# A hybrid decoder layer on one core: the Mixer's first projections on x without 1/rms, the last norm in a written order, one statistic moved

## The chip, the cores and the metric

The kernel runs on one core of a Trainium2 chip. The metric is the device time of one execution in microseconds; the time before is the median of three runs.

## The reference

x is 1024 positions of 1024 channels, all in float32. One layer is

```
x = x + 0.5 * SwiGLU_1(RMSNorm(x))
x = x + W_out concat[ GLA heads(RMSNorm(x)), short-conv groups(RMSNorm(x)) ]
x = x + 0.5 * SwiGLU_2(RMSNorm(x))
return RMSNorm(x)

RMSNorm(x)  = x * rsqrt(mean(x*x) + 1e-6) * gain
SwiGLU(h)   = (silu(h @ w_gate) * (h @ w_up)) @ w_down          # width 2816
proj        = h @ w_in  ->  q, k, v, g, a_lr, u, gate_b, gate_c
logg        = log_sigmoid(a_lr @ w_a2 + b_a) / 16               # the decay
o           = gated linear attention of q, k, v, logg, in chunks of 64; normed, times silu(g)
z           = gate_b * causal_conv(gate_c * u)                  # 3 taps
```

The layer is run once (DEPTH is 1). What matters below: 1/rms is one number per position and multiplies h, so it can be multiplied into a projection's result as well as into its operand.

## The kernel before, in words

x lies in SBUF as eight tiles of 128 channels by 1024 positions (`xs`), and the work goes over two halves of 512 positions. Every product is made of three TensorE passes: both operands are split into a high and a low part, and hi*hi, hi*lo and lo*hi are added (`PASSES`). A split is one cast on ScalarE (`S.copy`) and one subtraction, on VectorE as a rule.

Three stages follow each other. **FFN1** (class `Ffn`) runs its products in blocks of Strassen's form; its last block, `down_last` (L787 on), runs plainly: for half 0 and then half 1, over eight groups d of 128 channels, six matmuls of 128x512 each, then VectorE adds 0.5 times the sum to x (L802). The **Mixer** makes for each half: the decay (`project_decay`), k, q, v, u/c/b of the convolution, g, and the attention between them; then `out_proj` (L1203). **FFN2** is like FFN1, with the final norm at the end. Its `down_last` goes over three ranges of positions, 512, 256 and 256 wide (`tail`).

A norm is the class `Norm`. `add(k)` squares x's tile k on ScalarE and adds it to a running sum; the engine of the sum is `chain` (V is VectorE, G is GpSimd, none is VectorE and GpSimd in turns). `fin` then puts the sum through TensorE against ones (the statistic, L326), takes rsqrt on VectorE and GpSimd, spreads it as a diagonal (dg, L343) and multiplies that with ones on TensorE (rb, L347), which leaves 1/rms in every partition. `raw` (L355) multiplies x, gain and 1/rms in one VectorE instruction; `norm_h` splits the result into h's two parts.

The order of the work is made in three ways. A counter of modelled time, `clock`, is moved on by `tick(us)` after each step, and generators that were `spawn`ed with a wait are resumed when it has passed (`finish` resumes all to their ends). `pump` takes steps from a list of weight loads and splits as buffers come free: `plan_unit` puts a load (SyncE's queue), a cast (ScalarE) and a subtraction (VectorE) on it for each weight unit. Then a scheduler orders what each engine got, except where `in_order` pins the written order. At the end of FFN1, `finish()` and `in_order(f1.end, ...)` close the stage before the Mixer is built: half 0's norm is spawned 4.0 us after its last block, half 1's when the Mixer starts.

At the change from Mixer to FFN2 half 0 is normed beside `out_proj` of half 1, and `second` makes half 1's norm and operands while FFN2's first matmuls (`plain`, L482) run on half 0. At the end of FFN2 the three ranges are normed in turn: `first` multiplies range 0 on GpSimd (L1357), `scaled` multiplies ranges 1 and 2 on VectorE, `store` issues the transfers of the result on the queues of SyncE and ScalarE by turns.

Of the kernel before, what the change touches and what calls it, by code (L numbers as in the profile page):

```python
# [14 lines left out]
ALU = mybir.AluOpType  # L15
# [40 lines left out]
def trunk(ctx: ExitStack, tc: tile.TileContext, a, out):  # L56
# [60 lines left out]
    def pump(n=None):  # L117
        while todo and n != 0:
            n = n and n - 1
            tag, step = todo[0]  # L120
            if not tag():
                return
            todo.popleft()
            step()
# [81 lines left out]
    def plan_unit(src):  # L206

        st = {}
        key = ("u", units[0])
        units[0] += 1  # L210

        def load():
            st[0] = room("wr", "raw")
            nc.sync.dma_start(out=st[0], in_=src)

        def high():
            st[1] = room("wo", "whi", F32R)
            S.copy(st[1], st[0])  # L218

        def low():  # L220
            lo = room("wo", "wlo", F32R)
            sub(V, lo, st[0], st[1].bitcast(F32))
            free("wr")
            ready[key] = (st[1], lo)

        todo.extend([(room_for("wr"), load), (room_for("wo"), high), (room_for("wo"), low)])

    units, taken = [0], [0]
# [16 lines left out]
    def tick(us):  # L245
        pump()
# [41 lines left out]
    class Norm:  # L288
# [22 lines left out]

        def sum(self):
# [15 lines left out]
        def fin(self, bank, keep=True, waits=(2.7, 1.3), fill=lambda: None):  # L328

            n = self.n  # L330
            while self.late:
                self.sum()
# [37 lines left out]
    class Ffn:  # L370
# [411 lines left out]
        def down_last(self, after, ranges):  # L782
# [4 lines left out]
            rts = [[operand("ao", "act", x) for x in (r11, r21)], [operand("ao", "act", r12), None]]  # L787
            for n, (c, w) in enumerate(ranges):
                h, o = divmod(c, HALF)
                for d in range(KT):  # L790
                    if n == 1 and d == 0:
                        rts[1][1] = operand("ao", "act", r22)
# [13 lines left out]
                    tick(1.36 * w / HALF)  # L806
# [28 lines left out]
    def mixer_plans():  # L835
# [8 lines left out]
        for n in range(2):  # L844
            if n == 1:
                conv(0)
            group("k")
            group("q")
            for kq in range(4):
                plan_unit(a["w_v"][kq])  # L850
            if n == 0:
                conv(0)
            conv(1)
            group("g", 0)
            group("g", 1)
# [6 lines left out]
    class Mixer:  # L862
        def __init__(self, es):
            pool = lambda n, b, **k: es.enter_context(tc.tile_pool(name=n, bufs=b, reuse_waits="tile", **k))
            self.gp, self.sp = pool("gp", 9), pool("sp", 2)
            self.pp = pool("pp", 8, space=bass.MemoryType.PSUM)
# [12 lines left out]
            G.memset(self.state, 0.0)  # L879

# [25 lines left out]
        def project_decay(self, h):  # L906
# [237 lines left out]
        def attention(self, n, r):  # L1144
            yield 0.0
# [25 lines left out]
        def mix(self, n, h, front):  # L1171
# [9 lines left out]
            dec = self.project_decay(h)  # L1181
            next(dec)
            r["k"] = self.project_fm("k", h)
            r["b"] = next(dec)
            r["q"] = self.project_fm("q", h)
            spawn(self.attention(n, r))
# [27 lines left out]
    def norm_h(norm, h, bank, keep=True):  # L1214

        yield from norm.fin(bank, keep)
        hi, lo = (hp.tile([P, KT, HALF], F32R, tag="h", name=nm("h")) for _ in range(2))
# [40 lines left out]
    n2 = [Norm(0), Norm(HALF, chain=G)]  # L1258
# [43 lines left out]
    em = ExitStack()  # L1302
    m = Mixer(em)
    spawn(norm_h(n2[1], hm[1], m.bank), 3.0)
# [18 lines left out]
    m.out_proj(1, m1["act"], to_ffn2)  # L1323
    finish()
# [4 lines left out]
    f2.side = second(f2, n3[1], 0.0)  # L1329
    spawn(f2.side)  # L1330

    def store(n, k, y):

        c, w = tail[n]
# [123 lines left out]
```

## Time and profile before

| | |
|---|---|
| median of 3 runs | 1793.51 us (1792.5 to 1793.72) |
| the profiled execution's own time | 1794.18 us |
| its span in the profile | 1792.4 us, granted clock 0.983 |
| PE (TensorE matmul) busy | 1740.0 us, 97% |
| DVE (VectorE) busy | 1373.2 us, 77% |
| ACT (ScalarE) busy | 830.8 us, 46% |
| POOL (GpSimd) busy | 627.3 us, 35% |
| chain of work that ended last | PE 89%, issue 5%, DVE 4%, ACT 1%, POOL 1% |

All times are in microseconds from the span's start. "L802" is line 802 of the kernel. A view by windows gives busy time of each engine in a stretch, with the number of instructions in brackets, then TensorE's granted clock as a share of full speed. The timeline gives an engine's instructions in order, with the idle time ahead of each and what released it in square brackets. A PE that counts as busy isn't thereby at full speed: the granted clock tells that.

### The profile page before, as it was taken

Reading aid. Unit: us, or ns where it says so; the run is one execution under the profiler, and the core shown is the slowest. Engines: PE = TensorE matmul, PEld = TensorE weight load, DVE = VectorE, ACT = ScalarE, POOL = GpSimd, SP = SyncE. Lnnn points to the kernel's source line nnn. Section 1 sums busy time; section 2 is a strip of 40 time slices with the busy share of each in tenths; the row PEclk is TensorE's granted clock in tenths of the full one; section 3 lists DMA queues with packets and bytes.
Section 4 is the critical chain, followed back from the end, with each engine's and each line's share of the span. In section 5 each row is a group of like instructions: output and inputs, shape, how many; then the busy total and the mean of one; then the engine's idle time right before and its main releaser. Section 6 shows DMA issues by size and latency. Waiting matters only on the chain.

```text
span 1792.4 us, 21018 instructions
## 1 busy us (share of the span) xinstructions
PE 1740.0 (97%) x7814; PEld 1432.2 (80%) x7814; DVE 1373.2 (77%) x1847; ACT 830.8 (46%) x1442; POOL 627.3 (35%) x425
## 2 busy tenths in 40 slices
PE   8989999999999998899999999999999999999995
PEld 7768888888888875788888887888888888888884
DVE  6898778877798775775746668787788777987786
ACT  5464445554455444432442444354455544554453
POOL 0044354534444242220211020533545344543533
PEclk9999999999999998999999999999999999999997
DMA  5011212111111211222222222112111111112102
GB/s 214 1 47 47 71 47 63 54 49 61 58 48 47 71 53 47 83 83 82 70 84 90 77 73 92 34 36 71 48 59 52 55 59 59 47 48 71 48 24 94
DMA packets 35110, 112.92 MB, mean 63 GB/s; under 512 B 4384, under 2 KB 6848, under 8 KB 35008
## 3 DMA queue, kind: packets, MB, share of 16 engines
q1 hardware_dynamic: 32944, 108.42, 19.0%
q10 hardware_dynamic: 2064, 3.16, 0.5%
q8 instruction: 61, 1.00, 0.2%
q14 instruction: 41, 0.34, 0.1%
HBM read 107.37 MB, written 4.19 MB: 62 GB/s over the span
## 4 chain that ended last, share of the span: by engine, by line
PE 89%; issue 5%; DVE 4%; ACT 1%; POOL 1%; DMA 0%; ACTq 0%; POOLq 0%; DVEq 0%
PE ps L364 41%; PE ps L779 20%; PE pj L898 12%; PE dn L1203 5%; PE ps L482 2%; PE v L953 2%; PE ps L799 2%; PE sc L1022 1%; PE ps L506 1%; DVE sq L88 1%; PE alr L916 0%; DVE x L715 0%; DVE hraw L355 0%; DVE act L85 0%; DVE x L802 0%
## 5 line engine op out<-in xcount | busy, mean ns | idle before, releaser
L364 PE MATMUL ps<-R,w 128*128 128x512 f32 x1872 | 443.9, 391 | 3.4 <-DVE x L715 2.4
L364 PEld LDWEIGHTS ps<-R,w 128*128 128x128 f32 x1872 | 352.8, 189 | 78.0 <-DVE x L715 2.8
L779 PE MATMUL ps<-act,w 128*128 128x512 f32 x1680 | 386.3, 390 | 0.7 <-DVE x L715 0.7
L779 PEld LDWEIGHTS ps<-act,w 128*128 128x128 f32 x1680 | 313.7, 188 | 70.1 <-DVE act L701 4.4
L85 DVE TENSOR_TENSOR w<-raw,w 128x512 fp32r<-128x512 f32 x311 | 292.3, 946 | 78.7 <-ACT w L92 78.7
L364 PE MATMUL ps<-S,w 128*128 128x512 f32 x1404 | 331.4, 389 | 1.2 <-ACT w L92 1.2
L364 PEld LDWEIGHTS ps<-S,w 128*128 128x128 f32 x1404 | 263.6, 188 | 56.8 <-ACT w L92 1.7
L85 POOL TENSOR_TENSOR raw<-raw 128x512 f32<-128x512 f32 x59 | 77.3, 1309 | 597.4 <-DVE w L85 597.4
L92 ACT CAST w<-raw 128x512 fp32r<-128x512 f32 x311 | 192.2, 619 | 174.9 <-POOL raw L85 75.9
L88 POOL TENSOR_TENSOR x<-x,dx 128x512 f32<-128x512 f32 x160 | 265.7, 1697 | 17.5 <-ACT dx L766 17.5
L715 DVE SCALAR_TENSOR_TENSOR x<-ps,x 128x512 f32<-128x512 f32 x320 | 210.2, 682 | 20.7 <-PE ps L779 20.7
L898 PE MATMUL pj<-h,whi 128*128 128x512 f32 x640 | 200.4, 394 | 0.0
L85 DVE TENSOR_TENSOR wlo<-raw,whi 128x1024 fp32r<-128x1024 f32 x64 | 80.8, 1262 | 88.9 <-PE pj L898 47.4
L898 PEld LDWEIGHTS pj<-h,whi 128*128 128x128 f32 x640 | 119.0, 189 | 26.4 <-issue 1.9
L85 DVE TENSOR_TENSOR w<-T,w 128x512 fp32r<-128x512 f32 x118 | 102.4, 868 | 38.1 <-ACT w L92 38.1
L218 ACT CAST whi<-raw 128x1024 fp32r<-128x1024 f32 x64 | 67.0, 1046 | 138.7 <-PE pj L898 81.8
L898 PE MATMUL pj<-h,wlo 128*128 128x512 f32 x320 | 124.9, 390 | 0.0
L85 DVE TENSOR_TENSOR act<-act,act 128x512 fp32r<-128x512 f32 x103 | 109.8, 1069 | 13.1 <-ACT act L92 13.1
L92 ACT CAST act<-act 128x512 fp32r<-128x512 f32 x103 | 63.7, 621 | 75.7 <-PE ps L779 46.9
L92 ACT CAST w<-T 128x512 fp32r<-128x512 f32 x118 | 73.3, 621 | 53.6 <-PE ps L364 32.0
L85 POOL TENSOR_TENSOR raw<-raw,raw 128x512 f32<-128x512 f32 x59 | 95.5, 1619 | 4.6
L85 DVE TENSOR_TENSOR T<-raw,raw 128x512 f32<-128x512 f32 x59 | 49.5, 840 | 53.0 <-POOL raw L85 53.0
(196 smaller groups left out, 2152.3 us busy)
## 6 DMA issues: line engine op xcount, KB each, us to landing
raw<-in_ffn_w SPq DMA_DIRECT2D x86, 512.0 KB, 3.6
raw<-in_ffn_wd SPq DMA_DIRECT2D x44, 512.0 KB, 3.7
raw<-in_w_fm SPq DMA_DIRECT2D x40, 512.0 KB, 3.5
raw<-in_w_out SPq DMA_DIRECT2D x16, 512.0 KB, 3.6
x<-in_x SPq DMA_DIRECT2D x16, 256.0 KB, 6.1
raw<-in_w_v SPq DMA_DIRECT2D x8, 512.0 KB, 3.5
raw<-in_ffn_w ACTq DMA_DIRECT2D x2, 512.0 KB, 6.0
out<-y SPq DMA_DIRECT2D x2, 512.0 KB, 2.8
```

The source lines that it names most:

```text
L85: eng.tensor_tensor(o, x, y, op=ALU.subtract)
L88: eng.tensor_tensor(o, x, y, op=ALU.add)
L92: S.copy(hi, src)
L218: S.copy(st[1], st[0])
L364: nc.tensor.matmul(ps, lt[:, c:c + P], rk[j], start=(start and n == 0), stop=(n == last), skip_group_check=True)
L482: nc.tensor.matmul(pss[m], lts[m][:, c:c + P], rk[j], start=(q == 0 and k == 0 and t == 0), stop=(q == 1 and k == 3 and t == 2))
L715: V.scalar_tensor_tensor(xh(d, n), ps, 0.5, xh(d, n), op0=ALU.mult, op1=ALU.add)
L779: nc.tensor.matmul(ps, l2[i], r[0][j], start=(start and n == 0), stop=(n == 2), skip_group_check=True)
L799: nc.tensor.matmul(ps, l2[i], rts[h][q][:, 512 * j + o:512 * j + o + w], start=(q == 0 and k == 0), stop=(q == 1 and k == 2))
L898: nc.tensor.matmul(pss[f], w[i][:, k, f * P:(f + 1) * P], h[j][:, 4 * kh + k, :], start=(kh == 0 and k == 0 and n == 0), stop=(kh == 1 and ...
L953: nc.tensor.matmul(pss[t], h[i][:, kk, t * P:(t + 1) * P], u[j][:, k * 512:(k + 1) * 512], start=(kk == 0 and i == 0 and j == 0), stop=(kk ...
L1203: nc.tensor.matmul(pss[j], w[p][:, f * 512 + j * P:f * 512 + (j + 1) * P], act[q][i][:, f * 512:(f + 1) * 512], start=(i == 0 and f == 0 a ...
```

## The change

1. **From FFN1 to the Mixer.** The Mixer's tiles are made before FFN1's `down_last`. Half 0's q, k and decay projections are one new function, `project_qk`, on gain*x (tiles xg: the high part from ScalarE, the low part from VectorE, one instruction each) and not on h. Their 112 matmuls run in eight steps of 14. Beside each step lie the parts of x for the next ones (`x_part`), half 1's square of that step with its addition, and one step of `pump`. 1/rms is multiplied in when the results leave PSUM. The statistic of half 0 stands inside half 1's blocks of `down_last` (d = 4, 6, 7), its sum is now on GpSimd (`chain=G`), and h of half 0, which v, u/c/b and g still need, is made beside q and k. Half 1's h is spawned 28.0 us later. `plan_unit` takes several sources and loads four ahead; q's weights lie in Mixer tiles; `pump(n)` no longer counts loads.
2. **`down_last`.** The splits of its operands r12 and r22 stand at d = 2 and d = 4 of half 0; r22's stood at the start of half 1.
3. **From the Mixer to FFN2.** Half 1's sum of squares is closed before `finish`, and `second` waits 5.4 where it waited 0.0.
4. **The end.** The final norm is written into the blocks of the last two ranges (`last`); results go to two large tiles; of range 0's eight GpSimd multiplications four stand in range 2 and four behind the last statistic; transfers are grouped anew.

The core of the diff:

```diff
@@ class Norm: @@
+        def flush(self):
+            while self.late:
+                self.sum()
@@ down_last @@
-            rts = [[operand("ao", "act", x) for x in (r11, r21)], [operand("ao", "act", r12), None]]
+            rts = [[operand("ao", "act", x) for x in (r11, r21)], []]
...
-                    if n == 1 and d == 0:
-                        rts[1][1] = operand("ao", "act", r22)
+                    if n == 0 and d == 2:
+                        rts[1].append(operand("ao", "act", r12))
+                    if n == 0 and d == 4:
+                        t = mix[0].gl("act", F32R) if self.i == 1 else hp.tile([P, 4, 1024], F32R, tag="h", name=nm("act"))[:, 0, :]
+                        split(r22, t[:, 0:512], t[:, 512:1024])
+                        rts[1].append(t)
...
-                    tick(1.36 * w / HALF)
+                    tick(1.36 * w / HALF, int(self.i == 2 or (n, d) in ((0, 7), (1, 0), (1, 2), (1, 4), (1, 7))))
@@ class Mixer: @@
+        def project_qk(self, x, norm, wa, r):
+            pss = {(s, f): self.bank("pj") for s in "qk" for f in range(2)}
+            pa = self.bank("alr")
+            x_part(1, 1)
+            for kh in range(2):
+                w = {s: [u.rearrange("p (k c) -> p k c", k=4) for u in need(("u", 2 * kh + (s == "k")))] for s in "qk"}
+                for k in range(4):
+                    kk = 4 * kh + k
+                    for s, f in pss:
+                        for n, (i, j) in enumerate(PASSES):
+                            nc.tensor.matmul(pss[s, f], w[s][i][:, k, f * P:(f + 1) * P], x[j][:, kk, :],
+                                             start=(kk == 0 and n == 0), stop=(kk == KT - 1 and n == 2))
+                    for j in range(2):
+                        nc.tensor.matmul(pa, wa[:, kk, :], x[j][:, kk, :], start=(kk == 0 and j == 0),
+                                         stop=(kk == KT - 1 and j == 1))
+                    x_part(kk + 2, 0)
+                    n2[1].add(kk)
+                    if kk:
+                        x_part(kk + 1, 1)
+                    if k == 3:
+                        retire()
+                    tick(3.2, 1)
+            taken[0] = 4
+            r["dec"] = self.decay(pa, norm.r)
+            next(r["dec"])
+            for s in "qk":
+                r[s] = self.gl(s)
+            for s, f in pss:
+                V.scalar_tensor_tensor(r[s][:, f * 512:(f + 1) * 512], pss[s, f], DK ** -0.5 if s == "q" else 1.0, norm.r,
+                                       op0=ALU.mult, op1=ALU.mult)
@@ mix @@
+            else:
+                self.project_qk(self.x, n2[0], self.wa, r)
+                in_order(f1.end, nc.tensor, V, S, G)
+                spawn(self.attention(n, r))
@@ trunk @@
-    n2 = [Norm(0), Norm(HALF, chain=G)]
+    n2 = [Norm(0, chain=G), Norm(HALF, chain=G)]
...
+    def x_part(k, part):
+        if k >= KT:
+            return
+        hi, lo = (t[:, k, :] for t in mix[0].x)
+        if part == 0:
+            S.mul(hi, xh(k, 0), gains[:, 1, k:k + 1])
+        else:
+            V.scalar_tensor_tensor(lo, xh(k, 0), gains[:, 1, k:k + 1], hi.bitcast(F32), op0=ALU.mult, op1=ALU.subtract)
+
     def to_mix(n, d):
-        n2[n].add(d)
-        if n == 0 and d == KT - 1:
-            spawn(norm_h(n2[0], hm[0], f1.bank_norm, False), 4.0)
-
-    f1.run(to_mix, eh.close, halves)
-    finish()
-    in_order(f1.end, nc.tensor, V, S, G)
+        if n == 0:
+            n2[0].add(d)
+        elif d == 0:
+            n2[0].flush()
+        elif d in (4, 6, 7):
+            next(h0)
+        if n == 1 and d >= 6:
+            x_part(d - 6, 0)
+        if n == 1 and d == 7:
+            x_part(0, 1)
...
+    f1.run(to_mix, to_mixer, halves)
+    spawn(h0)
...
-    spawn(norm_h(n2[1], hm[1], m.bank), 3.0)
+    spawn(norm_h(n2[1], hm[1], m.bank, pause=1.0), 28.0)
...
+    n3[1].flush()
     finish()
...
-    f2.side = second(f2, n3[1], 0.0)
+    f2.side = second(f2, n3[1], 5.4)
...
     def last(n, d):
         n4[n].add(d)
-        if d < KT - 1:
-            return
-        if n == 0:
-            spawn(first(), 4.0)
-        elif n == 1:
-            spawn(second_range(), 2.6)
-        else:
+        if n and d == 0:
+            n4[n - 1].flush()
+        if (n, d) in ((1, 4), (1, 6), (2, 0)):
+            next(fins[0], None)
+        if (n, d) in ((2, 4), (2, 6), (2, 7)):
+            next(fins[1], None)
+        if n == 2 and d % 2:
+            y_of(0, d // 2)
...
```

**PE, the end of FFN1's `down_last`.** Each row is one group of matmuls; ps is a PSUM bank, act and w are operand and weight, alr the decay's bank, pj a bank of q or k. Before:

```order
L799 MATMUL ps_5369<-act_5181,w_5135 128x512 x3
L799 MATMUL ps_5369<-act_5270,w_5152 128x512 x3
L799 MATMUL ps_5384<-act_5181,w_5135 128x512 x3
L799 MATMUL ps_5384<-act_5270,w_5152 128x512 x3
L916 MATMUL alr_5452<-h_5346,wa_5448 128x512
L916 MATMUL alr_5452<-h_5347,wa_5448 128x512
```

In the change:

```order
L815 MATMUL ps_5376<-act_5236,w_5135 128x512 x3
L815 MATMUL ps_5376<-act_5261,w_5152 128x512 x3
L815 MATMUL ps_5387<-act_5236,w_5135 128x512 x3
L815 MATMUL ps_5387<-act_5261,w_5152 128x512 x3
L359 MATMUL ps_5395<-dg_5384,ones 128x512
L938 MATMUL pj_5409<-xg_5208,whi_5308 128x512
L938 MATMUL pj_5409<-xg_5209,whi_5308 128x512
L938 MATMUL pj_5409<-xg_5208,wlo_5319 128x512
L938 MATMUL pj_5410<-xg_5208,whi_5308 128x512
L938 MATMUL pj_5410<-xg_5209,whi_5308 128x512
```

Where the decay's matmuls on h came next, rb (dg times ones) and the 112 matmuls on xg now do; the statistic that belongs to this rb stands three blocks further up.

**PE, around z, the decay's second product (128x512 twice).** Before, z stands inside k and q, ahead of all of v:

```order
L898 MATMUL pj_5473<-h_5347,whi_5329 128x512
L898 MATMUL pj_5473<-h_5346,wlo_5395 128x512
L924 MATMUL z_5548<-b_5469,w_a_5442 128x512
L924 MATMUL z_5551<-b_5469,w_a_5442 128x512
L898 MATMUL pj_5568<-h_5346,whi_5399 128x512
L898 MATMUL pj_5568<-h_5347,whi_5399 128x512
L898 MATMUL pj_5568<-h_5346,wlo_5498 128x512
```

In the change:

```order
L1016 MATMUL v_5624<-wlo_5539,h_5434 128x512
L1016 MATMUL v_5624<-whi_5514,h_5435 128x512
L339 MATMUL st_5656<-ones,sq_5430 128x2 x4
L987 MATMUL z_5665<-b_5613,w_a_5198 128x512
L987 MATMUL z_5668<-b_5613,w_a_5198 128x512
L1016 MATMUL v_5624<-whi_5564,h_5434 128x512
L1016 MATMUL v_5624<-wlo_5609,h_5434 128x512
L1016 MATMUL v_5624<-whi_5564,h_5435 128x512
```

z now stands behind 42 of v's 96 matmuls, and behind half 1's statistic (st); 54 of v's matmuls lie between it and the first scores.

**PE, the start of FFN2.** R and w are operand and weight of FFN2's first products, `L326` and `L339` the statistic of half 1. Before:

```order
L482 MATMUL ps_8497<-R_8294,w_8382 128x512 x3
L482 MATMUL ps_8498<-R_8294,w_8418 128x512 x3
L482 MATMUL ps_8497<-R_8294,w_8382 128x512 x3
L482 MATMUL ps_8498<-R_8294,w_8418 128x512 x3
L326 MATMUL ps_8532<-ones,sq_8346 128x2 x4
L482 MATMUL ps_8497<-R_8294,w_8382 128x512 x3
L482 MATMUL ps_8498<-R_8294,w_8418 128x512 x3
```

In the change:

```order
L494 MATMUL ps_8518<-R_8314,w_8402 128x512 x3
L494 MATMUL ps_8519<-R_8314,w_8438 128x512 x3
L494 MATMUL ps_8518<-R_8314,w_8402 128x512 x3
L494 MATMUL ps_8519<-R_8314,w_8438 128x512 x3
L494 MATMUL ps_8518<-R_8444,w_8441 128x512 x3
L494 MATMUL ps_8519<-R_8444,w_8489 128x512 x3
L339 MATMUL ps_8570<-ones,sq_8366 128x2 x4
L494 MATMUL ps_8518<-R_8444,w_8441 128x512 x3
```

The statistic stands behind ten of the rows with three matmuls each, where it stood behind four.

## Rows read from the trace of the kernel before

**Rows 1.** The page's busy times of the engines over the span

```profile
PE 1740.0 (97%) x7814; PEld 1432.2 (80%) x7814; DVE 1373.2 (77%) x1847; ACT 830.8 (46%) x1442; POOL 627.3 (35%) x425
```

**Rows 2.** Windows: stretch, engines' busy us (instructions), granted clock, DMA share, GB/s

```profile
662.10:673.00 10.90, 7.92 (x36) 5.80 (x35) 6.14 (x11) 3.50 (x6) 3.34 (x3) 1.00 0.00 0
...
673.00:684.00 11.00, 7.82 (x25) 5.56 (x24) 9.68 (x11) 4.05 (x8) 4.95 (x4) 0.84 0.14 48
...
684.00:695.00 11.00, 7.07 (x15) 3.99 (x16) 9.03 (x13) 5.04 (x9) 2.67 (x2) 0.69 0.16 49
...
728.00:739.00 11.00, 7.56 (x26) 6.10 (x27) 10.96 (x16) 7.97 (x13) 0.00 (x0) 0.84 0.31 96
...
1122.70:1130.00 7.30, 7.30 (x22) 5.63 (x22) 1.46 (x3) 0.00 (x0) 2.80 (x3) 0.63 0.08 34
...
1778.70:1785.00 6.30, 2.19 (x6) 1.43 (x6) 4.44 (x11) 1.64 (x3) 4.20 (x4) 0.50 0.57 207
...
1785.00:1792.40 7.40, 0.04 (x1) 0.00 (x0) 4.03 (x10) 0.00 (x0) 0.00 (x0) 0.50 0.76 249
```

**Rows 3.** Chain of work that ended last: start, us, engine, tile, line, count

```profile
651.22 10.31 PE ps L799 x45
...
748.75 1.78 PE sc L1022 x16
...
750.53 10.90 PE pj L898 x48
```

**Rows 4.** Timeline of PE from FFN1's end to the first scores

```profile
667.80 1.05 PE L326 MATMUL ps<-ones,sq 128*128 128x2 f32 x8 [1.38 <-DVE sq L88]
...
706.44 1.98 PE L924 MATMUL z<-b,w_a 32*128 32x512 f32 x4
...
731.44 0.50 PE L953 MATMUL v<-wlo,h 128*128 128x512 f32 x1 [4.66 <-DVE wlo L85]
...
732.78 0.63 PE L953 MATMUL v<-whi,h 128*128 128x512 f32 x1
```

**Rows 5.** Timeline of DVE in the same stretch

```profile
677.20 1.41 DVE L355 SCALAR_TENSOR_TENSOR hraw<-x,gains,ps 128x512 f32<-128x512 f32 x2 [0.62 <-PE ps L347]
...
678.63 0.69 DVE L85 TENSOR_TENSOR h<-hraw,h 128x512 fp32r<-128x512 f32 x1
...
681.35 1.46 DVE L85 TENSOR_TENSOR h<-hraw,h 128x512 fp32r<-128x512 f32 x1 [0.61 <-ACT h L92]
...
716.26 1.22 DVE L85 TENSOR_TENSOR wlo<-raw,whi 128x1024 fp32r<-128x1024 f32 x1
...
717.39 2.63 DVE L933 TENSOR_TENSOR_SCAN b<-ones,e 128x128 f32<-128x128 f32 x8
...
719.94 9.11 DVE L355 SCALAR_TENSOR_TENSOR hraw<-x,gains,rb 128x512 f32<-128x512 f32 x6
...
735.46 1.37 DVE L1051 TENSOR_TENSOR zq<-zz,q 64x512 f32<-64x512 f32 x2
```

**Rows 6.** Timeline of POOL in the same stretch

```profile
680.95 1.30 POOL L88 TENSOR_TENSOR sq<-sq,sq 128x512 f32<-128x512 f32 x1 [2.21 <-ACT sq L303]
...
720.17 7.00 POOL L1031 TENSOR_TENSOR zz<-b 128x1024 f32<-128x1024 f32 x3 [15.13 <-DVE b L933]
```

**Rows 7.** Timeline of ACT in the same stretch

```profile
707.98 1.27 ACT L925 ACTIVATE b<-z,b_a 128x512 f32<-128x512 f32 x2
```

**Rows 8.** Timeline of PE at FFN2's start

```profile
1121.07 1.76 PE L326 MATMUL ps<-ones,sq 128*128 128x2 f32 x8 [4.14 <-DVE sq L88]
...
1122.70 6.86 PE L482 MATMUL ps<-R,w 128*128 128x512 f32 x18
```

**Rows 9.** Timeline of PE and DVE in the last two ranges

```profile
1753.15 2.66 PE L799 MATMUL ps<-act,w 128*128 128x256 f32 x20 [0.38 <-DVE act L85]
...
1778.29 0.41 DVE L802 SCALAR_TENSOR_TENSOR x<-ps,x 128x256 f32<-128x256 f32 x1
```

**Rows 10.** Transfers from 1765 to 1793 in 40 slices

```profile
GB/s 0 0 0 0 0 0 0 0 313 395 41 0 0 0 0 202 380 167 0 0 0 0 360 380 236 148 155 372 350 350 272 250 312 338 326 322 323 1 0 0
```

More of the change, by code (lines that the diff above doesn't have):

```diff
@@ L118, in pump @@
         while todo and n != 0:
-            n = n and n - 1
             tag, step = todo[0]
@@ L122, in pump @@
                 return
+            if n and step.__name__ != "load":
+                n -= 1
             todo.popleft()
@@ L204, in plan_plain, with plan_unit, load, high @@
             part(n, name, *where[name])
[L206 to L228, printed above, removed]
+    def plan_unit(*srcs, ahead=1):
+        loads, splits = [], []
+        for src in srcs:
+            st = {"key": ("u", units[0])}
+            units[0] += 1
+            src, mixer = src if isinstance(src, tuple) else (src, False)
+            when = (lambda: bool(mix)) if mixer else room_for("wo")
+            place = (lambda s: mix[0].gl(s, F32R)) if mixer else (lambda s: room("wo", s, F32R))
+            def load(st=st, src=src):
+                st[0] = room("wr", "raw")
+                nc.sync.dma_start(out=st[0], in_=src)
+            def high(st=st, place=place):
+                st[1] = place("whi")
+                S.copy(st[1], st[0])
+            def low(st=st, place=place):
+                lo = place("wlo")
+                sub(V, lo, st[0], st[1].bitcast(F32))
+                free("wr")
+                ready[st["key"]] = (st[1], lo)
+            loads.append((room_for("wr"), load))
+            splits.append([(when, high), (when, low)])
+        todo.extend(loads[:ahead])
+        for i, s in enumerate(splits):
+            todo.extend(s + loads[i + ahead:i + ahead + 1])
+    units, taken, mix = [0], [0], []
     def take():
@@ L330, in fin @@
             n = self.n
-            while self.late:
-                self.sum()
+            self.flush()
             st = bank("st")
@@ L879, in __init__, with banks @@
             G.memset(self.state, 0.0)
+        def banks(self, es):
+            self.pp = es.enter_context(tc.tile_pool(name="pp", bufs=8, reuse_waits="tile", space=bass.MemoryType.PSUM))
         def bank(self, s):
@@ L1349, in first @@
-    def first():
-        yield from n4[0].fin(f2.bank_norm)
-        for k in range(0, KT, 2):
-            y = room("wr", "y")
-            for i in range(2):
-                xg, yv = t2("xg"), y[:, i * HALF:(i + 1) * HALF]
-                S.mul(xg, n4[0].x(k + i), gains[:, 3, k + i:k + i + 1])
-                G.tensor_tensor(yv, xg, n4[0].r, op=ALU.mult)
-            store(0, k, y.rearrange("p (i c) -> p i c", i=2))
-            yield 1.3
-    def second_range():
-        yield from n4[1].fin(f2.bank_norm, False, (2.0, 1.3))
+    ys = []
@@ new lines, in y_of @@
+    def y_of(n, k):
+        if not ys:
+            y0, y1 = (hp.tile([P, KT, HALF], F32, tag="h", name=nm("y")) for _ in range(2))
+            ys.extend([y0, y1[:, :, 0:256], y1[:, :, 256:512]])
+        y = ys[n][:, k, :]
+        if n == 0:
+            S.mul(y, n4[0].x(k), gains[:, 3, k:k + 1])
+            G.tensor_tensor(y, y, n4[0].r, op=ALU.mult)
+        else:
+            n4[n].raw(y, 3, k)
+        m = (2, 4, 2)[n]
+        if k % m == m - 1:
+            c, w = tail[n]
+            eng = nc.scalar if n == 2 and k % 4 == 3 else nc.sync
+            k0 = k - m + 1
+            eng.dma_start(out=out[k0 * P:(k + 1) * P, c:c + w].rearrange("(i p) c -> p i c", p=P), in_=ys[n][:, k0:k + 1, :])
```

96 lines of the change are left out of this document (53 added, 43 removed).

## The prediction

> **What bounds the kernel now.** I read the page's busy times first: TensorE's matmuls are busy 1740.0 of 1792.4 us [rows 1]. A change that takes no matmuls away can win only where PE waits, or where it counts as busy at half clock. So the windows come next: cut the span into stretches of about 11 us and look for those where PE isn't full or its granted clock is below 1.00. Apart from the opening, which the change leaves alone, there are three places [rows 2]: the end of FFN1 with the Mixer's start (662 to 695 and 728 to 739), the start of FFN2 (1117 to 1130), and the last two ranges (from 1751 on). The change has one part for each. The chain of waits then gives each place its length, and the timelines of the engines say what PE waited for there.
>
> At full clock a 128x512 matmul takes 10.90 / 48 = 0.227 us [rows 3]; at half clock its starts lie 0.42 apart (731.44, then 732.78 and on) [rows 4]. The windows at clock 0.84 and 0.69 follow waits of PE [rows 2], so a wait costs its length and then more: a mean of 0.84 over 11 us is 3.5 us at half clock.
>
> **Place 1, from `down_last` of FFN1 to the first scores.** Before: 748.75 - 651.22 = 97.5 us on the chain [rows 3]. In that stretch PE waits for the statistic of half 0, for its rsqrt and diagonal, for the splits of h (the decay needs all eight tiles of h), and at 731.44 for 4.66 us on a weight split of v that stands on VectorE behind six hraw [rows 4, 5]. The change takes 1/rms out of the path: q, k and decay need only gain*x, and each tile of x is final when its own block has run. I add up what PE has to do now:
> - 93 matmuls of `down_last` left at 651.22 (45 of half 0, 48 of half 1), 93 x 0.227 = 21.1, and the statistic between them, 0.9 (8 short ones, 1.05 with the clock down [rows 4]): 22.0.
> - rb and the wait for the first low part of xg, which follows the last add to x by a cast and a subtraction (0.64 and 0.69 [rows 5, 7]): 1.4.
> - 112 matmuls of q, k and decay, 25.4, and 8 of v that the scheduler put among them, 1.8.
> - A loss to VectorE in these eight steps. It has 21.7 us of its own there (eight low parts of xg, eight hraw and eight lows of h at 0.69 to 0.73, four weight splits at 1.22 [rows 5], and four evacuations), against PE's 27.2. That would fit. But half 1's seven additions now run on POOL beside it, and the trace shows what this does: the same subtraction for h takes 0.69 alone and 1.46 while POOL adds squares at 680.95 [rows 5, 6], and six hraw with rb in SBUF beside zz take 9.11, 1.52 each, against 0.71 with rb in PSUM [rows 5, 6]. With 0.8 to 1.0 for each addition VectorE stands at about 28, 0.8 to 1 above PE; with its uneven steps I put 1.7.
>
> That is 52.3 us to the end of q and k. From there the order has 34 matmuls of v (7.7), half 1's statistic (0.9) and z (1.98 at [rows 4], 1.9 taken): z ends at 62.8. Then 54 matmuls of v (12.3, 12.7 with their evacuation) bring PE to the first scores at 75.5.
>
> But the scores need the decay's own chain after z. From the first b to the end of the scan it took 12.0 us before (707.98 to 720.02 [rows 5, 7]); without the weight split of 1.22 inside it and with a cast waiting on ScalarE I take 11.5. Then zz on POOL (7.00 / 3 = 2.3 [rows 6]), two exponentials of 0.62, three products of 0.68 (as zq [rows 5]), and 0.4 of hops: 17.5. Before, z ended 40 us ahead of the scores and all of this was covered. Now 12.7 us of v cover it: **scores at 62.8 + 17.5 = 80.3, a new wait of 4.8**, and some 2 us at half clock after it: 82.4. The place wins 97.5 - 82.4 = **15**. Its bounds: 22 if the wait doesn't come, 8 if VectorE sets the pace of q and k.
>
> One rule of the Trainium skill speaks against this part. Its page "SBUF — State Buffer", section "Who interferes with whom", says that a VectorE instruction with two inputs in SBUF and a GpSimd instruction that reads SBUF share a port by an exclusive lock, so that the later one stands still. Rows 5 and 6 agree, the hraw with a PSUM input included, which wasn't held. Taken literally, seven additions of 1.30 would block VectorE for 9.1 us, put it at 30.8 against PE's 27.2, and make the loss 3.6 in place of 1.7. I keep the rows' sum, since they show less than the whole addition lost each time.
>
> Where h goes: half 0's eight hraw and splits are no longer ahead of any matmul but those of v, 8 of which stand early; they lie beside q and k in the sum above. The 28.0 us by which half 1's h is put off cost nothing, since its first use is 40 us behind the scores; without that cover it would be 6 us of VectorE. The moved split of r22 takes a wait of about a microsecond from the start of half 1 and lies beside half 0's matmuls; it is in the 22.0. The loads of weights are the same in number and four are now queued ahead on SyncE; the DMA share here is at most 0.31 [rows 2], so I price that at nothing, and at 1 us if a load stands behind others.
>
> **Place 2, FFN2's start.** PE waits 4.14 us for the sum of half 1's squares, runs the statistic in 1.76, and then 18 matmuls in 6.86 [rows 8], against 18 x 0.227 = 4.1 at full clock: 4.14 + 0.8 + 2.7 = 7.6 lost, in a window of granted clock 0.63 [rows 2]. Now 18 more matmuls stand ahead of the statistic, 4.1 us of work, about as long as the wait. I leave 0.3 for it and 0.3 for rb, whose rsqrt stands on POOL behind other work: **7.0**. Bounds: 7.7, and 3 if the sum is late by as much again.
>
> **Place 3, the end.** The last add to x ends at 1778.70 [rows 9], 13.7 us before the span's end. PE has 96 narrow matmuls there, from 1750.7: at 2.66 / 20 = 0.133 [rows 9] that is 12.8, with statistics and rb of two ranges 3.6, and one add of 0.41: 1767.5 when nothing waits. The statistics of ranges 0 and 1 now stand some blocks further down, where their sums are done, and only four of POOL's multiplications lie beside them. If the chain behind the last add stays at 13.7, the end is at 1781.2. The transfers give nearly the same: some 3.0 of 4.2 MB are left from 1770.3, at 320 GB/s (mean of the last ten full slices [rows 10]) 9.4 us and 2 for the last issue and landing: 1781.7. I take 1781.4, **11** less. Bounds: 14 if the chain shrinks (8 products of range 2 follow rb, where ten y did), 6 if POOL's multiplications hold VectorE as before.
>
> **The sum.** 15 + 7 + 11 = 33: span 1792.4 - 33 = 1759.4. The profiled execution took 1794.18, 1.78 above its span: 1761.2. It lay 0.67 above the median of the runs: 1760.5.
>
> **The rivals.**
> - *No wait at the scores.* If the scheduled order gives the decay chain ScalarE and VectorE at once (its parts alone are some 14 us, against 12.7 of cover), place 1 wins 22: 40 in all, 1753.5. Against it: casts of weights stand in ScalarE's queue in the same stretch. Chance 0.20.
> - *VectorE paces q and k.* If every addition on POOL holds it for a full 1.3 and steps slip, place 1 wins 8: 26 in all, 1767.5. For it are 9.68 and 9.03 of 11 us busy before [rows 2] with less work in the same stretch. The rule of the Trainium skill named above would make this case the likelier one. Chance 0.13.
> - *Slower.* Each step of 14 matmuls waits for its low part of xg. If each such wait leaves PE at half clock, all of q, k, decay and v (216 matmuls with the last 8 of `down_last`) run at 0.42, 0.2 more each: +43, against 33 won: 1803. It decides from about 165 of the 216 on. For it: after a wait of 4.66 the matmuls were 0.42 apart, and the window shows 3.5 us of it [rows 2, 4]. Against it: the waits expected here are under 0.3 each. Chance 0.05.
> - *The waits only move.* Each part leaves PE's work as it is; should v wait for h, FFN2 for rb and the end for POOL, the three gains would be handed on to the next product, within 0.2% (3.6 us, about what a measurement of this kernel can tell from no change). Chance 0.03.
> - The forecast itself: 0.59.
>
> Of the 0.92 for faster all cases lie under 1775. The range takes the first two rivals and the bounds of the places (savings of 43 and of 18 in the span, so 1749.4 and 1774.4, and 1.1 from the span to the median): 1750 to 1775.
>
> **What would show it.** Right: a PE full at clock 1.00 from 651 to about 704, with no stretch at 0.84 or 0.69; then one wait of about 5 us at the first scores, released by a VectorE product; at FFN2's start no wait over 0.5 ahead of the statistic; the last add to x at about 1745 of a span of 1759, 14 us from the end, and transfers at over 300 GB/s to its end. Wrong: gaps in front of the matmuls on xg in each step; low parts of xg over 1 us each; POOL's y beside the last statistic; or a wait at v for h.

## The result, and the profile after

The changed kernel takes 1768.74 us (median of 4 runs, 1766.87 to 1770.16) where the kernel before took 1793.62 in the same runs: a ratio of 0.9861, interval 0.9848 to 0.9873. It is 24.9 us faster; the forecast was 33, with 1760.5 in a range of 1750 to 1775. The profiled execution has a span of 1767.5 at a granted clock of 0.988.

The span falls into five stretches by PE's timeline, which bound the three places: the start of FFN1's `down_last`, the start of the second scores (so that the half clock behind the first ones is counted), the last matmul of `out_proj`, the start of FFN2's `down_last`, and the end.

| | before | after | gain | forecast |
|---|---|---|---|---|
| opening and FFN1 | 647.66 | 646.91 | 0.75 | 0 |
| place 1, to the second scores | 113.61 | 101.07 | 12.5 | 15 |
| the rest of the Mixer | 352.94 | 352.95 | 0 | 0 |
| place 2, `out_proj`'s end to FFN2's `down_last` | 622.25 | 618.91 | 3.3 | 7 |
| place 3, to the end | 55.94 | 47.66 | 8.3 | 11 |

Windows of the profile after (stretch, busy us of PE, PEld, DVE, ACT and POOL with instructions, granted clock, DMA share, GB/s):

```profile
662.10:673.00 10.90, 10.88 (x52) 8.75 (x51) 8.17 (x12) 2.62 (x4) 6.61 (x4) 1.00 0.30 96
673.00:684.00 11.00, 10.94 (x47) 8.45 (x46) 9.75 (x12) 9.43 (x16) 2.93 (x2) 1.00 0.16 49
684.00:695.00 11.00, 10.62 (x47) 8.49 (x46) 11.00 (x11) 6.37 (x10) 5.40 (x3) 1.00 0.20 63
695.00:706.00 11.00, 11.00 (x50) 9.10 (x49) 10.10 (x13) 2.92 (x5) 3.98 (x2) 1.00 0.23 79
...
717.00:728.00 11.00, 8.76 (x37) 6.58 (x35) 5.57 (x11) 7.52 (x11) 4.04 (x2) 1.00 0.22 75
728.00:739.00 11.00, 6.62 (x25) 6.03 (x26) 10.94 (x10) 6.57 (x12) 5.25 (x4) 0.53 0.16 49
```

Where [rows 2] had 7.92, 7.82 and 7.07 busy of 11 at clocks down to 0.69, PE is now busy for at least 10.6 of 11 at clock 1.00 in these windows. Then, from 717 on, come a wait and a window at 0.53. PE's timeline says where:

```profile
673.16 1.36 PE L938 MATMUL pj<-xg,whi 128*128 128x512 f32 x2
...
701.38 0.62 PE L941 MATMUL alr<-xg,wa 128*128 128x512 f32 x2
...
710.42 1.98 PE L987 MATMUL z<-b,w_a 32*128 32x512 f32 x4
...
725.38 0.39 PE L1016 MATMUL v<-whi,h 128*128 128x512 f32 x1
732.38 3.76 PE L1085 MATMUL sc<-zq,zz 128*128 128x128 f32 x16 [6.62 <-ACT zz L1097]
```

The matmuls on xg run from 673.16 to 701.8, z follows at 710.42, v ends at 725.8, and the first scores wait 6.62 us. The profile puts that wait down to an exponential on ScalarE (L1097). But the second zq on VectorE ends at 732.24, 0.14 ahead of the scores; in the run e5 below it ends 0.16 ahead of them, and the third exponential of L1097 starts only after they have begun. So the scores wait for zq. VectorE and, in the second fence, GpSimd in the same stretch:

```profile
689.23 1.78 DVE L1373 SCALAR_TENSOR_TENSOR xg<-x,gains,xg 128x512 fp32r<-128x512 f32 x1
690.93 2.31 DVE L85 TENSOR_TENSOR wlo<-raw,whi 128x1024 fp32r<-128x1024 f32 x1
693.17 0.74 DVE L367 SCALAR_TENSOR_TENSOR hraw<-x,gains,rb 128x512 f32<-128x512 f32 x1
...
727.40 1.74 DVE L1106 TENSOR_TENSOR zz<-zz,k 128x512 f32<-128x512 f32 x1 [2.46 <-ACT zz L1096]
729.07 3.17 DVE L1114 TENSOR_TENSOR zq<-zz,q 64x512 f32<-64x512 f32 x2
```

```profile
688.72 1.74 POOL L88 TENSOR_TENSOR sq<-sq,sq 128x512 f32<-128x512 f32 x1 [2.49 <-ACT sq L312]
...
723.97 7.00 POOL L1094 TENSOR_TENSOR zz<-b 128x1024 f32<-128x1024 f32 x3 [9.30 <-DVE b L996]
```

At 727.40 the product of zz and k takes 1.74 and at 729.07 the two zq take 3.17, while GpSimd works on zz. PE at place 2:

```profile
1107.78 1.05 PE L339 MATMUL ps<-ones,sq 128*128 128x2 f32 x8
...
1113.10 1.13 PE L359 MATMUL ps<-dg,ones 128*128 128x512 f32 x2
...
1154.13 4.60 PE L376 MATMUL ps<-S,w 128*128 128x512 f32 x12 [1.79 <-ACT ps L694]
```

The wait of 4.14 ahead of the statistic [rows 8] is gone. A wait of 1.79 is there 41 us behind rb, and 12 matmuls behind it take 4.60 in place of the 2.88 of full clock. The end, on VectorE, and the transfers in 40 slices of 0.7 us from 1740:

```profile
1750.54 0.41 DVE L818 SCALAR_TENSOR_TENSOR x<-ps,x 128x256 f32<-128x256 f32 x1
...
1754.71 1.48 DVE L355 TENSOR_TENSOR dg<-ident,rs 128x256 f32<-128x256 f32 x1
1756.11 4.77 DVE L367 SCALAR_TENSOR_TENSOR y<-x,gains,ps 128x256 f32<-128x256 f32 x12
```

```profile
GB/s 0 0 0 0 0 0 0 0 0 0 0 0 0 140 383 225 0 0 0 0 29 386 348 344 344 47 94 342 358 353 367 338 345 337 344 373 389 105 0 0
DMA packets 3232, 4.19 MB, mean 150 GB/s; under 512 B 160, under 2 KB 2208, under 8 KB 3232
```

The last add to x is at 1750.95 (1778.70 in [rows 9]), 16.6 us from the end and not 13.7.

### The profile page after: what moved, and what is told of

Its sections match the earlier page's. It is cut to its first block, busy times and chain, and to the rows that moved or that the text cites. A ratio compares the mean times of both kernels' runs of the same rounds, so it can differ in the third digit from the quotient of the medians.

```text
span 1767.5 us, 21020 instructions
## 1 busy us (share of the span) xinstructions
PE 1728.0 (98%) x7814; PEld 1425.9 (81%) x7814; DVE 1380.2 (78%) x1855; ACT 832.4 (47%) x1446; POOL 640.4 (36%) x430
## 4 chain that ended last, share of the span: by engine, by line
PE 87%; issue 5%; DVE 4%; ACT 2%; POOL 1%; DMA 0%; DVEq 0%; ACTq 0%; POOLq 0%
PE ps L376 41%; PE ps L791 21%; PE pj L919 11%; PE dn L1272 5%; PE ps L815 2%; PE v L1016 2%; PE sc L1085 2%; PE ps L518 1%; POOL hraw L85 1%; PE pj L938 1%; DVE hraw L367 1%; DVE x L727 0%; DVE sq L88 0%; PE o L1168 0%; DVE w L85 0%
## 5 line engine op out<-in xcount | busy, mean ns | idle before, releaser
L92 ACT CAST w<-raw 128x512 fp32r<-128x512 f32 x311 | 192.3, 620 | 175.7 <-POOL raw L85 75.5
L919 PE MATMUL pj<-h,whi 128*128 128x512 f32 x576 | 180.3, 395 | 0.0
L919 PEld LDWEIGHTS pj<-h,whi 128*128 128x128 f32 x576 | 107.3, 189 | 22.6 <-PE z L987 0.8
L919 PE MATMUL pj<-h,wlo 128*128 128x512 f32 x288 | 112.3, 391 | 0.0
```

Source lines behind the costliest of these rows:

```text
L92: S.copy(hi, src)
L919: nc.tensor.matmul(pss[f], w[i][:, k, f * P:(f + 1) * P], h[j][:, 4 * kh + k, :], start=(kh == 0 and k == 0 and n == 0), stop=(kh == 1 and ...
```

## The experiments

All are edits of the changed kernel; ratios are to the kernel before. Runs of the changed kernel differ by 3 us, and by the profiles nearly all such differences lie in the opening (see the last section), so the verdicts go by the stretches. By the totals alone only e1, e9 and e10 lie outside the changed kernel's interval of 0.9848 to 0.9873. Where nothing was edited the stretches repeat within 0.2 us, place 3 within 0.35, with two exceptions that lie in the clock behind a wait: 1.4 in place 1 of e3 (behind the same wait at the scores) and 1.5 in place 2 of e4c and e5 (last section). The Mixer's 1.2 in e4 and e10 and 0.5 in e5 follow from those edits (see there). No run undoes part 1 of the change as a whole; what it won is read from the profiles before and after:

| | median us | opening | place 1 | Mixer | place 2 | place 3 |
|---|---|---|---|---|---|---|
| after | 1768.74 | 646.91 | 101.07 | 352.95 | 618.91 | 47.66 |
| e1, old end | 1775.41 | 645.25 | 101.02 | 352.95 | 619.04 | 54.74 |
| e2, statistic early | 1770.42 | 645.24 | 100.91 | 352.94 | 621.85 | 47.66 |
| e3, four subtractions on VectorE | 1765.97 | 645.01 | 99.65 | 353.08 | 615.33 | 47.33 |
| e4, z first | 1768.21 | 647.79 | 99.57 | 354.10 | 619.02 | 47.62 |
| e4c, z behind 12 of v | 1763.78 | 645.37 | 96.80 | 352.94 | 617.42 | 47.67 |
| e5, zz on VectorE | 1764.98 (one run) | 646.80 | 97.95 | 353.42 | 617.36 | 47.67 |
| e6, squares' sum on VectorE | 1773.23 (one run) | 643.85 | 108.01 | 352.94 | 618.98 | 47.72 |
| e7, six products early | 1770.91 (one run) | 648.04 | 101.03 | 352.94 | 618.95 | 48.14 |
| e8, two transfers left out | 1766.09 (one run) | 646.42 | 101.05 | 352.94 | 618.98 | 44.91 |
| e9, e3 with e4c | 1760.34 | 645.26 | 96.77 | 352.94 | 615.35 | 47.48 |
| e10, e9 with e5 | 1759.13 | 647.81 | 94.05 | 354.12 | 615.27 | 47.35 |

**The end put back (e1).** `store`, `scaled`, `first`, `second_range` and `last` as before.

> The changed kernel with the final norm, the result's tiles and the transfers as they were before (part 4 undone). Between 1737.30 and the end of the profile before and 1720.68 and the end of the profile after, 8.3 us of the gain lie in this part. Theory: the parts add up, so undoing this one alone costs 8.3 and gives about 1777. Rival: part of those 8.3 comes from the operand splits of down_last that were moved earlier (part 2, kept here) and the old end keeps some of it: 1771 to 1774.

Measured: 54.74 for the end, 7.1 more than after; ratio 0.9900 (0.9879 to 0.9921). Part 4 is worth 7.1 of the 8.3, and 1.2 (55.94 to 54.74) stays without it: the rival holds for that much. In PE's timeline the waits of 1.73 and 0.38 for operands at the start of the second range before are gone in e1, and the wait ahead of the statistic behind them has grown from 1.45 to 2.91.

**The statistic put back (e2).**

```diff
-    f2.side = second(f2, n3[1], 5.4)
+    f2.side = second(f2, n3[1], 0.0)
```

> The changed kernel with the wait of `second` back from 5.4 to 0.0, so that the statistic of half 1 stands behind four rows of FFN2's matmuls again. Theory: the work behind rb (hraw, sums and splits of half 1's operands, among them eight subtractions on GpSimd) had about 2 us of slack before and lost 4.1 when 18 matmuls were put ahead of rb; so the 1.79 us wait at 1154.13 and the half clock behind it go, the 4.1 us wait ahead of the statistic comes back with its half clock, and the net is +3.3: about 1772. Rival: the wait at 1154.13 has another cause, and undoing the move costs the whole 7.0: about 1775.7.

Measured: place 2 at 621.85, +2.9, and 1770.42 (ratio 0.9869, 0.9851 to 0.9888): the theory. PE's timeline of this run has the 4.14 us wait again, and no wait at the copies:

```profile
1105.95 1.86 PE L339 MATMUL ps<-ones,sq 128*128 128x2 f32 x8 [4.14 <-DVE sq L88]
...
1156.87 2.88 PE L376 MATMUL ps<-S,w 128*128 128x512 f32 x12
```

**Four subtractions moved (e3).**

```diff
@@ half1 @@
-                sub(G, raws[1, k], raws[1, k], r[1, k])
+                sub(V, raws[1, k], raws[1, k], r[1, k])
```

> The changed kernel with four of the eight subtractions that make half 1's operands for S3 and S4 on VectorE in place of GpSimd. Theory: GpSimd's run of eight (18.71 us from 1130.63, 2.34 each) ends last and holds ScalarE's casts and with them the copy of PSUM for which PE waits 1.79 us at 1154.13; with half of them on VectorE (0.68 each) the wait and the half clock behind it go: -3.7, about 1765. Rival: the copy stands in ScalarE's queue behind casts that wait for something else: no change, 1768.7.

Measured: place 2 at 615.33, -3.6; 1765.97 (0.9839, 0.9819 to 0.9858). First GpSimd's run in the kernel after, then in e3, and e3's PE:

```profile
1130.63 18.71 POOL L85 TENSOR_TENSOR hraw<-hraw,hraw 128x512 f32<-128x512 f32 x8 [18.31 <-DVE hraw L85]
```

```profile
1127.45 14.61 POOL L85 TENSOR_TENSOR hraw<-hraw,hraw 128x512 f32<-128x512 f32 x4 [18.32 <-DVE hraw L85]
```

```profile
1149.01 2.88 PE L376 MATMUL ps<-S,w 128*128 128x512 f32 x12
```

Four take 14.61 in place of 18.71 for eight (the first one alone stands for 9.51 in e3 and 7.70 after, see the last section), PE's wait and the half clock are gone, and place 2 wins 622.25 - 615.33 = 6.9: the 7.0 of the forecast. So 3.6 of the 7 had been handed on to the work behind rb.

**z right behind the decay (e4).**

```diff
@@ mix @@
                 in_order(f1.end, nc.tensor, V, S, G)
+                r["b"] = next(r.pop("dec"))
                 spawn(self.attention(n, r))
```

> The changed kernel with the decay's second product and what follows it written right behind q, k and decay, ahead of v: in PE's order z stands directly behind the last matmul of the decay and all 96 of v behind it. Theory: the 6.62 us wait at the first scores comes from z standing behind 42 of v's matmuls; with 96 matmuls (21.8 us) as cover for a chain of some 20 us it goes, with the 3.1 us of half clock behind it; in return PE waits about 2 us ahead of z for the evacuation of the decay and runs some 3 us at half clock: net -6, about 1762.5. Rival: what counts is the chain's own length, which GpSimd's subtractions draw out by holding VectorE's products; then a wait of over 3 us stays at the scores and the net is -2 to +1: 1767 to 1770.

Measured: place 1 at 99.57, only 1.5 less; 1768.21 (0.9854, 0.9835 to 0.9873). Neither theory had it whole. PE's timeline and two windows of this run:

```profile
704.37 3.18 PE L987 MATMUL z<-b,w_a 32*128 32x512 f32 x4 [1.83 <-DVE b L983]
...
734.68 1.95 PE L1085 MATMUL sc<-zq,zz 128*128 128x128 f32 x16
```

```profile
696.00:707.00 11.00, 9.05 (x31) 5.84 (x31) 10.15 (x13) 3.51 (x5) 6.67 (x5) 0.91 0.22 75
707.00:718.00 11.00, 11.00 (x42) 8.69 (x42) 3.83 (x10) 7.71 (x7) 0.00 (x0) 0.78 0.01 2
```

No wait is left at the scores, as the theory has it; but the wait of 1.83 ahead of z leaves the clock at a mean of 0.91 and then 0.78. By the two windows that is 2 x (0.09 + 0.22) x 11 = 6.8 us at half clock, a cost of 3.4. The scheduler no longer put 8 of v among q and k, and two more waits came there and in v: 1.11 and 0.47 for low parts of xg (0.39 after), and 1.10 for a weight split of v. The new waits and the clock take back about 7.5 of the 9.7 us that the wait at the scores and its clock had cost.

**z behind 12 of v (e4c).**

```diff
@@ project_v, behind the matmuls of weight unit kq and position tile t @@
+                    if (kq, t) == (0, 0) and "dec" in r:
+                        r["b"] = next(r.pop("dec"))
```

> The changed kernel with z asked for a little later than in the run before: written behind the first six of v's matmuls of the first weight unit, so that in PE's order 12 of v stand ahead of z and 84 behind it. Theory: the wait at the scores is a matter of z's place alone, and the run with z directly behind the decay lost its gain to a wait of 1.83 ahead of z and the half clock after it. With work in between neither wait is there: the stretch from down_last to the second scores falls from 101.1 to about 93 (6.6 of wait and some 2 of half clock less): 1760.5. Rival: the chain from z to the scores (20.0 in both runs) is too long for what is left of v, a wait of 2 or more stays at the scores with its half clock: 97 to 99, 1765 to 1767.

Measured: 96.80, -4.3; 1763.78 (0.9839, 0.9813 to 0.9864), between the two, nearer the rival. PE:

```profile
702.95 1.98 PE L987 MATMUL z<-b,w_a 32*128 32x512 f32 x4
...
726.20 1.39 PE L359 MATMUL rb<-dg,ones 128*128 128x512 f32 x2 [1.95 <-DVE dg L355]
...
728.67 2.75 PE L1087 MATMUL sc<-zq,zz 128*128 128x128 f32 x16
```

z waits for nothing and the scores for nothing. The longest wait that is left, 1.95, is ahead of rb of half 1. Its rsqrt stands on GpSimd behind two zz and is done at 722.73; its diagonal then stands on VectorE behind a product of zz and k that takes 2.36 (0.68 alone) beside the third zz, and starts at 725.47. The wait was moved again, to queues that the theory hadn't looked at.

**The first three zz on VectorE (e5).**

```diff
@@ gla_scores, onv is 3 for half 0 and 0 for half 1; attention @@
-                    G.tensor_tensor(zb, bb, bb[:, :, s - 1:s].to_broadcast([P, 512 // s, 2 * s]),
+                    (V if li < onv else G).tensor_tensor(zb, bb, bb[:, :, s - 1:s].to_broadcast([P, 512 // s, 2 * s]),
...
-            yield from self.gla_scores(r["at"], r["q"], r["k"], r["b"])
+            yield from self.gla_scores(r["at"], r["q"], r["k"], r["b"], 3 * (1 - n))
```

> The changed kernel with the first three subtractions zz of half 0 on VectorE in place of GpSimd. Theory: GpSimd's seven microseconds of zz beside VectorE's products hold these (zz times k 1.74 in place of 0.68, zq 3.17 for two in place of 1.37), 2.9 us of the 20 from z to the scores. Without them the products take 0.7 and 1.4 again; VectorE pays 3.7 for three subtractions where GpSimd took 2.3 for the first: scores 1.5 earlier, 1767. Rival: the products were late for another reason (ScalarE's exponentials, the copies of v); then they stay at 1.6 or more each and the scores come 1 us later.

```profile
724.80 3.49 DVE L1094 TENSOR_TENSOR zz<-b 128x1024 f32<-128x1024 f32 x3
728.20 0.68 DVE L1106 TENSOR_TENSOR zz<-zz,k 128x512 f32<-128x512 f32 x1
728.80 1.39 DVE L1114 TENSOR_TENSOR zq<-zz,q 64x512 f32<-64x512 f32 x2
```

The products take 0.68 and 1.39: they had been held by GpSimd, by 1.06 and 1.78. The wait at the scores falls from 6.62 to 4.64 and place 1 to 97.95: 3.1 less, of which 2.0 is the wait and 1.1 the clock behind it, where 1.5 was expected; 0.5 comes back in the rest of the Mixer (353.42).

**The squares' sum on VectorE (e6).**

```diff
-    n2 = [Norm(0, chain=G), Norm(HALF, chain=G)]
+    n2 = [Norm(0, chain=G), Norm(HALF, chain=V)]
```

> The changed kernel with half 1's seven additions of squares on VectorE in place of GpSimd. By the prediction's term VectorE loses 0.8 to 1.0 us for each addition on GpSimd; it gains these back (low parts of xg 0.74 in place of 1.78) and pays 0.69 for each addition. Theory: PE sets the pace of q and k (51.4 us from 650.47 to their end, no wait over 0.4), so nothing moves by more than 0.5 us. Rival: VectorE sets it, and q and k end 2 us earlier.

In the stretch of q and k both kernels begin the matmuls on xg 26.25 us behind `down_last`'s start. After, PE waits once in them, 0.39 for a low part of xg; here it doesn't wait at all (the scheduler put 16 of v among them in place of 8), and no instruction of VectorE is held. So at most 0.4 us were VectorE's doing, as the theory says. The total can't be used: the scheduler now put half 1's hraw ahead of the products for the scores, on VectorE's timeline

```profile
723.74 4.74 DVE L367 SCALAR_TENSOR_TENSOR hraw<-x,gains,rb 128x512 f32<-128x512 f32 x2
728.40 2.45 DVE L1106 TENSOR_TENSOR zz<-zz,k 128x512 f32<-128x512 f32 x1
730.78 4.05 DVE L367 SCALAR_TENSOR_TENSOR hraw<-x,gains,rb 128x512 f32<-128x512 f32 x6
734.75 1.40 DVE L1114 TENSOR_TENSOR zq<-zz,q 64x512 f32<-64x512 f32 x2
```

and the scores wait 13.80. A different order, not a different cost.

**Six products of range 0 early (e7)** (in `last`, `if n == 2 and d > 1: y_of(0, d - 2)`, and k from 6 behind the last statistic).

> The changed kernel with six of GpSimd's eight products of range 0 inside range 2 and two behind the last statistic, in place of four and four. Theory: the end is set by the transfers, of which 3.67 of 4.19 MB are left when the stretch of full load begins at 1754; two products earlier start 0.5 MB earlier, and the stretch from FFN2's down_last to the end falls from 47.7 by 1 to 1.5. Rival: the products hold VectorE's additions of squares (0.41 alone, 1.18 to 1.31 beside them), the last add to x is as much later, and nothing is won or 1 us lost.

Measured: 48.14, +0.5, which is the rival's outcome: the last add to x comes 1.1 later. The squares' last two additions, 0.41 each alone and 1.69 together after, take

```profile
1753.08 2.56 DVE L88 TENSOR_TENSOR sq<-sq,sq 128x256 f32<-128x256 f32 x2
```

and rb comes 2.0 later (38.35 behind `down_last`'s start, 36.40 after). That the end moves by 0.5 only says that the chain had at least 1.5 us to spare in the kernel after, and so wasn't what set its end. **Two transfers left out (e8)** (in `y_of`, `and not (n == 0 and k > 3)` on the condition of the issue) asks this directly.

> The changed kernel without the two transfers of range 0's last four tiles (1.05 of the 4.19 MB of the result are not written; all arithmetic stays). Theory: from the last add to x the end takes 16.6 us and not 13.7 because the transfers set it; with 1.05 MB less at some 350 GB/s the stretch from FFN2's down_last to the end falls by 2.9, from 47.7 to about 44.8, until VectorE's last product (6.6 us ahead of the end) with 3.3 us of issue and landing behind it sets the end at 44.4. Rival: the chain of the last statistic, its diagonal and VectorE's products sets the end, and leaving transfers out changes it by less than 0.5.

Measured: 44.91, -2.75, with VectorE's instructions where they were to within 0.04 us. The transfers set the end.

**Together (e9, e10).**

> The changed kernel with z behind 12 of v's matmuls and with four of half 1's eight subtractions on VectorE, two edits that were run one by one. Theory: they mend two places that don't touch each other, so the gains add: 96.8 for the stretch from down_last to the second scores and 615.3 from FFN2's start to its down_last, against 101.1 and 618.9: -7.9, about 1761 with the opening at its mean. Rival: the half clock behind the wait in FFN2 comes and goes from run to run, and what the second edit wins is the 2 us of the wait alone: -6.

Measured: 96.77 and 615.35, as in the single runs; 1760.34 (0.9816, 0.9796 to 0.9837).

> As the run before, with the first three zz of half 0 on VectorE too. Theory: the stretch to the second scores has 1.95 us of wait left, ahead of rb, whose rsqrt stands on GpSimd behind the seven microseconds of zz; without these rb is in time, the products aren't held, and the stretch falls from 96.8 to about 94. Rival: VectorE's queue is the longer by 3.7 and the diagonal for rb stands behind the three zz; the wait stays and nothing is won.

Measured: 94.05; 1.2 of it comes back in the rest of the Mixer (354.12), between the second and the third scores: PE waits 0.85 us at 745.57 for a weight split on VectorE (0.86 at the same place in e4, none in e9). 1759.13 us, ratio 0.9809 (0.9794 to 0.9825): 9.6 below the changed kernel, and by that beyond its interval. PE has no wait at rb or the scores:

```profile
726.92 1.02 PE L359 MATMUL rb<-dg,ones 128*128 128x512 f32 x2
...
729.17 1.95 PE L1087 MATMUL sc<-zq,zz 128*128 128x128 f32 x16
```

## Why the prediction was right or wrong

The direction, the three places and the order of their sizes were right, and most terms: 93 matmuls with the statistic, the wait for xg, q and k to their end were put at 52.3 us and took 51.4; z ended at 61.9 by the trace and at 62.8 by the sum; v at 75.3 and 75.5. The last add to x was forecast 31.0 us behind the start of FFN2's `down_last` (1767.5 - 1736.46) and came 31.1 behind it. Three steps failed, all of them about what stands behind the part that was made faster. They cost 2.5, 3.7 and 2.7 us, each inside its place's bounds; the opening's 0.75, which no edit made, went the other way.

**Place 1, 15 against 12.5.** The new wait at the scores was named, at 4.8; it was 6.6. The step that was mis-sized is "three products of 0.68", 2.0 in all: they took 4.9, and the chain from z to the scores 20.0 in place of 17.5. The text had shown in [rows 5, 6] that six hraw beside zz take 1.52 each, and took the products alone; e5 puts the same three at 2.1. And "some 2 us at half clock" was 3.1 by the rows behind the wait: scores 3.76 for 1.78, the 48 matmuls 12.0 for 10.9 [rows 3]. The loss to VectorE, put at 1.7, was at most 0.4. (The 21.7 us of VectorE's own are 24 instructions at 0.70 and four splits at 1.22; the four evacuations named with them aren't in it, and came only behind the last matmul of q and k.)

**Place 2, 7 against 3.3.** The step "I leave 0.3 for it and 0.3 for rb" looked at the statistic and at rb, and not at what waits for rb. Putting 18 matmuls ahead of rb takes 4.1 us of cover from hraw, sums and splits of half 1. Before, the copy of PSUM ended at 1170.9, 1.5 ahead of the matmuls that need it; ScalarE's and PE's rows before:

```profile
1170.34 0.58 ACT L682 COPY ps<-ps 128x512 f32<-128x512 f32 x1
```

```profile
1172.45 2.88 PE L364 MATMUL ps<-S,w 128*128 128x512 f32 x12
```

After, PE waits 1.79 and pays 1.7 in half clock. e2 and e3 show it from both sides.

**Place 3, 11 against 8.3.** "If the chain behind the last add stays at 13.7" was one bound and "some 3.0 of 4.2 MB are left" the other. The second decides (e8), and its size was wrong: by the slices above only 140, 383 and 225 GB/s of 0.7 us, 0.52 MB, are out by 1751, and 3.67 MB were left at 1754, where the full load begins. At 350 GB/s that is 10.5 us, and 1.4 more lie in the two slices at 47 and 94, in which SyncE's queue waited for products.

**The rivals and the signs.** "No wait at the scores" is refuted by the 6.62; e4 shows that another place for z takes this wait away, at a price. "The waits only move" came true for 3.6 of place 2's 7. "VectorE paces q and k" gave 1767.5, close to what was measured, but isn't what happened: its stretch took 51.4 and not 59 (52.3 and the 7 that this rival wins less), and e6 finds 0.4 us in it. GpSimd's additions did hold VectorE, in seven instructions by 1.03 to 1.09 (xg 1.78 for 0.74, wlo 2.31 for 1.23), 7.4 us in all, more than the 0.8 to 1.0 each that was taken. By the Trainium skill's rule ("SBUF — State Buffer", "Who interferes with whom"), taken literally, they would have held it for 9.1. The forecast had 5.6 to 7.0, and the 7.4 is nearer to that. VectorE had room for it, so the time that the rule gave for the change wasn't right. The same rule of the Trainium skill, which the prediction weighed for the squares alone, agrees with the products at the scores: 4.9 beside GpSimd's zz, 2.1 without them (e5). "Slower" is refuted by the windows at clock 1.00. Two of the signs of being wrong were there all the same: two of the eight low parts of xg took 1.78, and with GpSimd's y beside the last statistic the diagonal took 1.48 at 1754.71, 0.41 at 1750.20.

## What to carry to other kernels

When a wait is taken away from a chain, everything behind it loses that much cover: ask of each result that now comes at another time who waits for it next, how much slack it had there, and on which queue it stands, before counting the whole wait as won. Here a late producer was best moved a few microseconds earlier with other matmuls between it and its input (e4c), not as early as possible (e4). Where two engines share work on SBUF, take the held price from the row that shows both, for each instruction that will stand beside the other, not for the ones being moved only.

## What the runs showed that was not expected

The same wait can cost the clock or not. The wait at the copies of place 2 was 1.79 to 1.82 us in eight of the profiles; in six of them, the one of after among them, the 12 matmuls behind it took 4.60 to 4.62, and in e4c and e5, at 1.79 too, 3.0, with the same code around it. From the profile of e5:

```profile
1151.38 3.01 PE L376 MATMUL ps<-S,w 128*128 128x512 f32 x12 [1.79 <-ACT ps L694]
```

Likewise the opening, which no edit touched, takes 643.85 to 648.04 us to the start of FFN1's `down_last`, and goes with the granted clock of its window from 30 to 60. From the profile after, and then from e6:

```profile
30.00:60.00 30.00, 25.02 (x97) 19.31 (x96) 22.15 (x37) 11.05 (x20) 1.01 (x1) 0.89 0.11 36
```

```profile
30.00:60.00 30.00, 24.39 (x105) 18.59 (x104) 23.80 (x38) 12.07 (x21) 1.01 (x1) 1.00 0.12 36
```

It is 1.00 at 643.85, 0.94 at 645.0 to 645.4, 0.89 at 646.4 to 648.0 and 0.83 at 646.8 to 647.8. This is nearly all of the spread between runs, and why 0.75 of the 24.9 us belong to no part of the change.

GpSimd pays too when it meets VectorE. The squares' additions beside q and k take up to 2.4 (the first of the two that begin at 695.24) in place of 1.30 [rows 6]. And the mean of a run of subtractions hides one long instruction. Half 1's subtractions by tile, as count and least, median and longest ns, in the kernel after and then in e3:

```profile
L85 POOL TENSOR_TENSOR hraw<-hraw,hraw x8: 1289/1736/7702, 1130.6 to 1147.6; 128x512 f32<-128x512 f32 x8
```

```profile
L85 POOL TENSOR_TENSOR hraw<-hraw,hraw x4: 1737/1740/9510, 1127.5 to 1140.3; 128x512 f32<-128x512 f32 x4
```

In e3 the long one is the first, from 1127.45 to 1136.96. VectorE's timeline of e3 beside the four:

```profile
1132.71 0.68 DVE L85 TENSOR_TENSOR S<-hraw,S 128x512 fp32r<-128x512 f32 x1
...
1137.44 1.77 DVE L85 TENSOR_TENSOR S<-hraw,S 128x512 fp32r<-128x512 f32 x1
```

From 1126.69 to 1137 VectorE's instructions follow each other without a gap, each at about 0.68, and none is held; the first of 1.77 comes at 1137.44, when GpSimd's others run. So a subtraction that takes at most 1.74 in the other three stood for 9.51 us beside a VectorE without a gap. The kernel after shows the same from 1130.63, with 7.70. In both it ends 1.23 us after the start of VectorE's only instruction there with an input in PSUM (sg, at 1135.73 and 1137.10); that this is what let it in is not shown. Work given to GpSimd beside a VectorE that doesn't pause can thus be late by most of that stretch, and a mean (2.3 for the eight, 3.7 for the four) doesn't show it.
